# Hybrid decoder trunk on one core: new step offsets for the phases of sliding attention and retention

## The chip, the cores and the metric

The kernel runs on one core of a Trainium2 chip. The metric is the device time of one execution in microseconds (us). Before the change the median of three runs is 1740.38 us (1739.54 to 1740.76). One more execution was profiled.

## What is computed

Two decoder layers over 512 tokens of width 1024. Each layer is a SwiGLU block, a hybrid mixer and a second SwiGLU block, each followed by a residual sum and a layer norm. The change lies in the mixer, which projects its input once into seven parts and feeds two groups of heads:

```python
def hybrid_mixer(x, w_in, w_out, sinks, rope_cos, rope_sin, ret_cos, ret_sin):
    h = x @ w_in
    qa, ka, va, qr, kr, vr, gr = jnp.split(h, IN_SPLITS, axis=-1)
    ...
    y_attn = sliding_window_sink_attention(qa, ka, va, sinks)   # 8 query heads, 2 key heads of 64
    ...
    y_ret = multiscale_retention(qr, kr, vr, gr)                # 8 heads of 64
    return jnp.concatenate([y_attn, y_ret], axis=-1) @ w_out
```

Sliding attention works on blocks of 128 tokens: a token group of 128 queries sees its own block and the one before it, masked to a window of 128 keys. Its softmax has a learned sink per head:

```python
m = jnp.maximum(jnp.max(s, axis=-1, keepdims=True), sink)
p = jnp.exp(s - m)
denom = jnp.sum(p, axis=-1, keepdims=True) + jnp.exp(sink - m)
o = jnp.einsum('bnhgqk,bnkhd->bnqhgd', (p / denom).astype(v.dtype), vv)
```

Retention is chunked by 128 tokens: decayed scores within a chunk, a state carried from chunk to chunk, a norm per head, and a gate.

## The kernel before

**Matmuls.** Every large matmul is done in three: each fp32 operand is split into a high and a low part (`split`, ScalarE writes the high part at line 175, VectorE the low part at line 176), and `mm3` (lines 190 to 192) adds high by high, high by low and low by high in one PSUM bank. These three lines are nearly all of TensorE's work. In the mixer they are the projections: `proj` gives a transposed projection of 512 tokens in 24 matmuls, `proj_tok` a projection of 128 tokens with 512 columns, also in 24.

**Steps.** The mixer's program is traced in one order by Python, and two kinds of work are woven together by a counter. `projs` and `proj_tok` call `self.step()` after each 12 matmuls, in the middle and at the end of a projection. `step` adds one to `now` and runs each waiting task whose time has come. A task is a generator; `yield w` sets its next time to `now + w`. `spawn(gen, delay)` sets its first. Within one step the tasks run in the order in which they were spawned. `finish` runs tasks to their end at once.

**Attention tasks.** After the first value projection of retention (line 947) four tasks are spawned, one for each token group n. A task has these phases:

- scores (line 1043): 24 matmuls with 64 rows of the array each, in four PSUM banks; then copies and masks into the tile `s` (lines 1046, 1048) and the softmax of the first key head (lines 1053 to 1066), all traced in the same step
- the softmax of the second key head, after the `yield` of line 1067 (3 steps)
- transposes (line 1073), after the same `yield`'s second turn (4 steps): 8 of 128 by 128 in two PSUM banks, with masks at line 1076
- values (line 1087), after the `yield` of line 1081 (2 steps): 8 matmuls with 64 columns of weights (4 for group 0) in one PSUM bank, then a split into `yah`, `yal`

**Retention tasks.** Four tasks for pairs of heads. Task p is spawned when its rotated queries and keys have been traced (line 962), with the delay `STEPS[p][0]`. Its phases on TensorE are the scores (line 1101, 16 matmuls with 64 rows) with key transposes (line 1112), then after `STEPS[p][1]` steps the states (line 1122, 6 matmuls, which read the decayed keys that VectorE wrote at line 1115), then after `STEPS[p][2]` steps the outputs (lines 1139 and 1135). The last phase, two steps later, works on VectorE and GpSimd alone and writes `O` (line 1159).

**What the end of the mixer waits for.** After the gate projections the output projection begins with the attention half of token groups 0 and 1 (`half(0, 0)`, `half(1, 0)`). The retention half of group 0 needs `O` times the gates (line 977), its transposes (line 490) and their split.

**What sets the order.** A scheduler lays out each engine's instructions by tracing order and readiness at build time. The splits and the `mm3` matmuls are kept behind the instruction that was traced before them on their engine; the matmuls of the tasks aren't. So the first projection matmul behind a step stands behind the last TensorE instruction that the step traced. Everything waits by semaphores. There are eight PSUM banks of one kind (`ps`), given out to projections and tasks alike. The tiles `s`, the transposed weights and the queries share a pool of eight (`t4k`), retention's tiles a pool of ten (`rr`).

Of the kernel before, what the change touches and what calls it, by code (L numbers as in the profile page):

```python
# [22 lines left out]
NT = SEQ // P  # L23
# [12 lines left out]
AHEAD = 8  # L36
LOOK = 6
DELAY = (5, 5, 9, 9)
STEPS = ((4, 2, 2), (3, 2, 3), (3, 3, 2), (3, 2, 2))

QA, KA, VA, QR, KR, VR, GR = 0, 512, 640, 768, 1280, 1792, 2304

# [57 lines left out]
class Trunk:  # L100
# [772 lines left out]
    def mixer(self, sinks, cst, g, b):  # L873
        nc, tc, W = self.nc, self.tc, self.W
        with ExitStack() as ctx:
# [64 lines left out]
            att, ret = [], []  # L940
            us = [W.get() for _ in range(4)]
            for t in range(NT):
                acc = self.ps()
                self.proj_tok(acc, us, t)
                if t == 0:
                    for n in range(NT):
                        att.append(self.spawn(self.attention(n), 5 * n))
                nc.scalar.copy(vr[:, t, :], acc)
            W.done(4)
            for pp in range(2):  # L950
                kq = [[None, None], [None, None]]
                for i in range(2):
                    for cc in range(2):
# [6 lines left out]
                        if i:  # L960
                            p = pp * 2 + cc
                            ret.append(self.spawn(self.retention(p, kq[cc][1], kq[cc][0]), STEPS[p][0]))

# [60 lines left out]
    def attention(self, n):  # L1024


        nc = self.nc
        c = self.c
        k0 = max(n - 1, 0) * P
        nk = (n + 1) * P - k0  # L1030
        nb = nk // P
        ns = slice(n * P, (n + 1) * P)
        mm = nc.tensor.matmul
        s = self.big([P, 8, P])
        over = c["over"].bitcast(mybir.dt.int32)[:, None, :].to_broadcast([P, 2, P])
        for c2 in range(2):
            sb = [self.ps().rearrange("p (c k) -> p c k", c=2) for _ in range(2)]
            q, k = self.qT[c2], self.kT
            for cc in range(2):
                for i, (qi, ki) in enumerate(((0, 0), (0, 1), (1, 0))):  # L1040
                    for kv in range(2):
                        pr = slice(kv * HD, (kv + 1) * HD)
                        mm(sb[kv][:, cc, :nk], q[qi][pr, cc, ns], k[ki][pr, k0 : k0 + nk], start=i == 0, stop=i == 2)  # L1043
            for kv in range(2):
                h0 = kv * 4 + c2 * 2
                nc.scalar.copy(s[:, h0 : h0 + 2, :], sb[kv][:, :, nk - P : nk])
                ahead = sb[kv][:, :, :P] if n else c["rsc"][:, 3:4, 4:5].to_broadcast([P, 2, P])
                nc.vector.copy_predicated(s[:, h0 : h0 + 2, :], over, ahead)
        for kv in range(2):
            hs = slice(kv * 4, kv * 4 + 4)  # L1050
            den = self.small.tile([P, 4], F32, tag="den", name=self.nm("den"))
            m = self.small.tile([P, 4], F32, tag="m", name=self.nm("m"))
            nc.vector.tensor_reduce(out=m, in_=s[:, hs, :], op=ALU.max, axis=AX.X)
            nc.vector.scalar_tensor_tensor(out=m, in0=m, scalar=-SCALE, in1=c["nsk"][:, hs], op0=ALU.mult, op1=ALU.min)
            es = self.small.tile([P, 4], F32, tag="es", name=self.nm("es"))
            nc.vector.tensor_add(es, m, c["sk"][:, hs])
            for cc in range(4):
                h = kv * 4 + cc
                nc.scalar.activation(s[:, h, :], s[:, h, :], AF.Exp, bias=m[:, cc : cc + 1], scale=SCALE,
                                     accum_out=den[:, cc : cc + 1])  # L1060
            nc.scalar.activation(es, es, AF.Exp)
            nc.vector.tensor_add(den, den, es)
            nc.vector.reciprocal(den, den)
            for cc in range(4):
                h = kv * 4 + cc
                nc.scalar.activation(s[:, h, :], s[:, h, :], AF.Copy, scale=den[:, cc : cc + 1])
            yield 3 + kv
        pT = []
        for kv in range(2):
            pT.append(self.big([P, 2, 512]))  # L1070
            tb = self.ps()
            for cc in range(4):
                nc.tensor.transpose(tb[:, cc * P : (cc + 1) * P], s[:, kv * 4 + cc, :], self.ident)  # L1073
            if n:
                for kb, mask in enumerate(("under", "causal")):
                    nc.vector.tensor_tensor(out=pT[kv][:, kb, :].rearrange("p (c q) -> p c q", c=4),
                                            in0=tb.rearrange("p (c q) -> p c q", c=4),
                                            in1=c[mask][:, None, :].to_broadcast([P, 4, P]), op=ALU.mult)
            else:
                nc.scalar.copy(pT[kv][:, 0, :], tb)  # L1080
        yield 2
        yb = self.ps()
        for kb in range(nb):
            blk = n - nb + 1 + kb
            for kv in range(2):
                cs = slice(kv * HD, (kv + 1) * HD)
                mm(yb[cs, :], self.va[:, blk, cs], pT[kv][:, kb, :], start=kb == 0, stop=kb == nb - 1)  # L1087
        self.split(self.ya[0][:, :, ns], self.ya[1][:, :, ns], yb.rearrange("p (c q) -> p c q", c=4))

    def retention(self, p, qT, kT):  # L1090
# [19 lines left out]
        for n in range(NT - 1):  # L1110
# [6 lines left out]
                                in1=wk[:, None, hp, None].to_broadcast([P, NT - 1, 2, HD]), op=ALU.mult)  # L1117
        yield STEPS[p][1]
        kvb = self.ps()
# [6 lines left out]
        for n in range(1, NT - 1):  # L1126
            nc.vector.scalar_tensor_tensor(out=st[:, n, :], in0=st[:, n - 1, :], scalar=g128[:, p : p + 1],
                                           in1=st[:, n, :], op0=ALU.mult, op1=ALU.add)
        yield STEPS[p][2]
        ob = self.ps()  # L1130
# [131 lines left out]
```

## Time and profile before

| | |
|---|---|
| median of three runs | 1740.38 us |
| profiled execution | 1738.96 us |
| its span, first to last instruction | 1737.2 us |
| mean granted TensorE clock | 0.999 |
| DMA, mean over the span | 126 GB/s |
| matmuls of lines 190 to 192 in the chain of work that ended last | 31% each |

Busy shares of the engines stand in the prediction. The chain of work that ended last is followed back from the last instruction: its pieces follow each other without a gap, so each piece's duration is what that piece costs the kernel, and groups of equal matmuls are given as one piece ("x8"). "PE ps L190" is a matmul of line 190 into a PSUM tile. A row of the timeline shows the start, the duration, the engine, the line, the operation and its tiles, and in brackets the idle time before it and what ended that. The list of waits shows who waited for whom: the sum in us, how often, the longest.

### The profile page before, as it was taken

Reading aid. Unit: us, or ns where it says so; the run is one execution under the profiler, and the core shown is the slowest. Engines: PE = TensorE matmul, PEld = TensorE weight load, DVE = VectorE, ACT = ScalarE, POOL = GpSimd, SP = SyncE. Lnnn points to the kernel's source line nnn. Section 1 sums busy time; section 2 is a strip of 40 time slices with the busy share of each in tenths; the row PEclk is TensorE's granted clock in tenths of the full one; section 3 lists DMA queues with packets and bytes.
Section 4 is the critical chain, followed back from the end, with each engine's and each line's share of the span. In section 5 each row is a group of like instructions: output and inputs, shape, how many; then the busy total and the mean of one; then the engine's idle time right before and its main releaser. Section 6 shows DMA issues by size and latency. Waiting matters only on the chain.

```text
span 1737.2 us, 29495 instructions
## 1 busy us (share of the span) xinstructions
PE 1726.2 (99%) x11998; PEld 1574.6 (91%) x11998; DVE 1432.8 (82%) x2041; ACT 965.4 (56%) x1587; POOL 189.7 (11%) x160
## 2 busy tenths in 40 slices
PE   9999999999999999999999999999999999999998
PEld 9999988897788999998899999889877899999886
DVE  7888888856867999878999988888568589888887
ACT  5465656378623655565555556554784246555651
POOL 0000022111211000014010000312011110000231
PEclk9999999999999999999999999999999999999999
DMA  6334389422223243279433324982323133334891
GB/s 194 98 98 138 130 205 203 132 86 80 67 97 74 98 143 101 98 216 214 139 74 130 114 98 158 214 198 92 106 77 98 49 94 126 98 109 137 212 211 49
DMA packets 167223, 219.52 MB, mean 126 GB/s; under 512 B 5296, under 2 KB 119984, under 8 KB 167088
## 3 DMA queue, kind: packets, MB, share of 16 engines
q1 hardware_dynamic: 142160, 172.55, 30.5%
q0 software_dynamic: 24928, 45.09, 14.5%
q8 instruction: 94, 1.54, 0.4%
q14 instruction: 41, 0.34, 0.1%
HBM read 212.38 MB, written 2.10 MB: 123 GB/s over the span
## 4 chain that ended last, share of the span: by engine, by line
PE 98%; DMA 1%; DVE 1%; ACT 0%; SPq 0%; POOLq 0%; issue 0%; DVEq 0%
PE ps L190 31%; PE ps L191 31%; PE ps L192 31%; PE ps L490 1%; DMA raw<-in_ffn_w_gu_dram 1%; PE ps L1087 1%; PE ps L1043 1%; PE ps L1139 1%; PE ps L1101 1%; PE ps L1073 0%; PE ps L1135 0%; PE ps L1122 0%; PE ps L462 0%; PE ps L1112 0%; DVE ul L176 0%; ACT uh L175 0%
## 5 line engine op out<-in xcount | busy, mean ns | idle before, releaser
L190 PE MATMUL ps<-xh,uh 128*128 128x256 f32 (+1 forms) x1544 | 449.6, 291 | 0.0
L192 PE MATMUL ps<-xh,ul 128*128 128x256 f32 (+1 forms) x1544 | 447.5, 290 | 0.4 <-DVE ul L176 0.4
L191 PE MATMUL ps<-xl,uh 128*128 128x256 f32 (+1 forms) x1544 | 447.3, 290 | 0.4 <-DVE xl L176 0.4
L175 ACT CAST uh<-raw 128x1024 fp32r<-128x1024 f32 (+1 forms) x274 | 234.2, 875 | 204.6 <-PE ps L191 102.5
L192 PE MATMUL ps<-Th,ul 128*128 128x256 f32 x1248 | 345.0, 276 | 0.0
L190 PE MATMUL ps<-Th,uh 128*128 128x256 f32 x1248 | 345.0, 276 | 0.0
L191 PE MATMUL ps<-Tl,uh 128*128 128x256 f32 x1248 | 345.0, 276 | 0.0
L176 DVE TENSOR_TENSOR ul<-raw,uh 128x1024 fp32r<-128x1024 f32 (+1 forms) x274 | 270.2, 1003 | 65.0 <-ACT uh L175 64.0
L190 PEld LDWEIGHTS ps<-xh,uh 128*128 128x128 f32 x1544 | 290.1, 188 | 8.6 <-issue 1.6
L192 PEld LDWEIGHTS ps<-xh,ul 128*128 128x128 f32 x1544 | 290.1, 188 | 8.2 <-DVE ul L176 0.9
L191 PEld LDWEIGHTS ps<-xl,uh 128*128 128x128 f32 x1544 | 291.0, 189 | 7.0 <-DVE xl L176 0.6
L190 PE MATMUL ps<-uh,xh 128*128 128x512 f32 x720 | 285.4, 396 | 0.5 <-ACT xh L175 0.5
L191 PE MATMUL ps<-ul,xh 128*128 128x512 f32 x720 | 282.9, 393 | 0.0
L192 PE MATMUL ps<-uh,xl 128*128 128x512 f32 x720 | 281.3, 391 | 0.0
L192 PEld LDWEIGHTS ps<-Th,ul 128*128 128x128 f32 x1248 | 234.4, 188 | 0.0
L191 PEld LDWEIGHTS ps<-Tl,uh 128*128 128x128 f32 x1248 | 234.4, 188 | 0.0
L190 PEld LDWEIGHTS ps<-Th,uh 128*128 128x128 f32 x1248 | 234.4, 188 | 0.0
L175 ACT CAST uh<-S 128x1024 fp32r<-128x1024 f32 x156 | 163.5, 1051 | 119.6 <-PE ps L191 110.0
L176 DVE TENSOR_TENSOR ul<-S,uh 128x1024 fp32r<-128x1024 f32 x156 | 190.5, 1223 | 35.1 <-ACT uh L175 34.8
L396 POOL DMA_DIRECT2D R<-in_ffn_w_down_dram x80 | 96.4, 1211 | 993.8 <-DVE ul L176 898.6
L176 DVE TENSOR_TENSOR ul<-R,uh 128x1024 fp32r<-128x1024 f32 x120 | 145.4, 1224 | 29.3 <-ACT uh L175 28.8
L175 ACT CAST uh<-R 128x1024 fp32r<-128x1024 f32 x120 | 124.8, 1047 | 71.6 <-DMA R<-in_ffn_w_down_dram 33.7
(160 smaller groups left out, 2430.7 us busy)
## 6 DMA issues: line engine op xcount, KB each, us to landing
raw<-in_ffn_w_gu_dram SPq DMA_DIRECT2D x86, 1024.0 KB, 5.8
R<-in_ffn_w_down_dram POOLq DMA_DIRECT2D x80, 512.0 KB, 7.5
raw<-in_w_in_dram SPq DMA_DIRECT2D x18, 1024.0 KB, 5.2
R<-in_ffn_w_down_dram SPq DMA_DIRECT2D x16, 1024.0 KB, 6.5
raw<-in_ffn_w_down_dram SPq DMA_DIRECT2D x12, 1024.0 KB, 7.7
R<-in_ffn_w_down_dram SPq DMA_DIRECT2D x8, 512.0 KB, 4.2
raw<-in_w_in_dram SPq DMA_DIRECT2D x8, 512.0 KB, 5.9
raw<-in_w_out_dram SPq DMA_DIRECT2D x8, 512.0 KB, 6.2
```

The source lines that it names most:

```text
L175: a = self.nc.scalar.copy(hi, src)
L176: b = self.low = self.nc.vector.tensor_sub(lo, src, hi.bitcast(F32))
L190: keep(mm(out, ah, bh, start=start, stop=False, **kw))
L191: keep(mm(out, ah, bl, start=False, stop=False, **kw))
L192: keep(mm(out, al, bh, start=False, stop=stop, **kw))
L396: self.nc.gpsimd.dma_start(src, rows(i, j, g * 2, 2), accum_op=ALU.add))
L490: nc.tensor.transpose(b[:, c * P : (c + 1) * P], src[:, c * P : (c + 1) * P], self.ident)
L1043: mm(sb[kv][:, cc, :nk], q[qi][pr, cc, ns], k[ki][pr, k0 : k0 + nk], start=i == 0, stop=i == 2)
L1087: mm(yb[cs, :], self.va[:, blk, cs], pT[kv][:, kb, :], start=kb == 0, stop=kb == nb - 1)
L1101: nc.tensor.matmul(sb[:, ns], kT[pr, ns], qT[pr, ns], start=True, stop=True)
L1139: ins = nc.tensor.matmul(ob[:, o0 : o0 + HD], ST[h][:, n, :], vr[:, n, p * P + h * HD : p * P + (h + 1) * HD], start=n == 0, stop=n == 0 o ...
```

## The change

The change edits four places, all of them numbers of steps:

```diff
-STEPS = ((4, 2, 2), (3, 2, 3), (3, 3, 2), (3, 2, 2))
+STEPS = ((5, 2, 2), (5, 2, 3), (4, 2, 2), (4, 2, 2))
...
                     for n in range(NT):
-                        att.append(self.spawn(self.attention(n), 5 * n))
+                        att.append(self.spawn(self.attention(n), 5 * n + 1))
...
-            yield 3 + kv
+            yield 2 + kv
         pT = []
...
-        yield 2
+        yield 5 if n < NT - 1 else 3
         yb = self.ps()
```

Attention's task n now starts at step 5n + 1 after the spawn, its second softmax follows two steps later, the transposes three after that, and the values five steps after the transposes, for the last group three. (Task 0 starts at step 1 either way, since a delay of 0 is seen by the next step only.) So from step 11 on the values of one group, the transposes of the next and the scores of the one after stand in one step. Retention's tasks 0, 2 and 3 start one step later, task 1 two; task 2 has two steps instead of three to its states. No instruction is added or removed.

## The prediction

> **What bounds the kernel now.** I read the page's busy shares first, then the chain of work that ended last, then the list of TensorE's waits, and last the chain inside the two mixer stages (372 to 530 us, and 1231 to 1390 us for layer 1), piece by piece.
>
> ```profile
> span 1737.2 us, 29495 instructions
> PE 1726.2 (99%) x11998; PEld 1574.6 (91%) x11998; DVE 1432.8 (82%) x2041; ACT 965.4 (56%) x1587; POOL 189.7 (11%) x160
> PE 98%; DMA 1%; DVE 1%; ACT 0%; SPq 0%; POOLq 0%; issue 0%; DVEq 0%
> PE ps L190 <- ACT xh L175: 0.5, 2, 0.2
> ```
>
> TensorE is busy 99% of the span and carries 98% of the chain. The only wait of TensorE that is charged to a mixer stage is the last row: 0.5 us, twice 0.2, at the first use of the gated retention output. So a mixer stage lasts as long as its matmuls take to stream, and the change, which removes no matmul, can act in two ways only: through what it costs TensorE to go from one kind of matmul to another, or through a wait that isn't there today.
>
> The profiled execution took 1738.96 us around its span of 1737.2 us; the median of the runs shown is 1740.38 us, 1.4 us more. I work out differences and add them to the median.
>
> **Where the groups stand.** One step is half a projection, 12 matmuls of lines 190 to 192. I counted steps from the spawn of the attention tasks (line 947), by hand, through `step`, and write S, T, V for the scores, transposes and values of a token group, A, B, C for retention's three TensorE phases (lines 1101 with 1112; 1122; 1135 with 1139).
>
> Before: S0 1, S1 5, T0 8, V0 S2 10, T1 12, V1 14, S3 15, A0 16, T2 A1 17, B0 18, V2 B1 19, C0 20, T3 C1 22, A2 23, V3 24, A3 25, B2 26, B3 27, C2 28, C3 29. That is 20 interruptions of the projections' stream a layer, and the chain below shows them in this order. After: S0 1, T0 S1 6, V0 T1 S2 11, V1 T2 S3 16, A0 17, B0 A1 19, V2 T3 C0 B1 21, V3 C1 A2 24, B2 A3 26, C2 B3 28, C3 30. That is 11. Inside a step the older task goes first, as V0 S2 and T2 A1 do now.
>
> **What an interruption costs.** Pieces of the chain (start, us on the chain, what), layer 0:
>
> ```profile
> 404.69 0.87 PE ps L1073 x8
> 405.57 0.24 PE ps L190
> 411.17 1.01 PE ps L1087 x4
> 412.18 1.63 PE ps L1043 x24
> 413.80 0.43 PE ps L190
> 426.08 1.87 PE ps L1087 x8
> 427.94 0.43 PE ps L190
> 430.94 1.63 PE ps L1043 x24
> 432.57 0.43 PE ps L190
> 435.57 1.09 PE ps L1101 x16
> 436.66 0.48 PE ps L1112 x3
> 437.14 0.24 PE ps L190
> 439.95 0.87 PE ps L1073 x8
> 440.82 1.09 PE ps L1101 x16
> 441.92 0.48 PE ps L1112 x3
> 442.39 0.23 PE ps L190
> 445.19 0.67 PE ps L1122 x6
> 445.86 0.23 PE ps L190
> 448.65 1.87 PE ps L1087 x8
> 450.52 0.86 PE ps L1122 x6
> 451.38 0.23 PE ps L190
> ```
>
> An undisturbed matmul of the stream takes 0.23. After T it takes 0.24, after A 0.24, after B 0.23: these groups leave nothing behind. After S and after V it takes 0.43, so each of these two costs 0.20 when the full array follows. Three shared steps exist already and show what sharing brings. T2 A1: 0.87, 1.09, 0.48, 0.23, each exactly what it is alone; sharing saved nothing. V2 B1: B takes 0.86 instead of 0.67, so V's 0.20 (here 0.19) moved from the stream's matmul to B; saved nothing. V0 S2: S takes its usual 1.63, and only one 0.43 follows; here 0.20 was saved, because V is followed directly by S, with no full-width matmul between.
>
> The Trainium skill, "TensorEngine Tiling (Array Packing)", section Key Properties, says that changing the tiling mode drains the TensorE. By that rule what counts is not interruptions but mode changes, and on my step lists these are 23 a layer before and 24 after, so the rule speaks against the change; the rows agree with it in kind (T and B, of full width, are free, V and S are not). Its sum would be that of the rows, one change more a layer.
>
> **The change part by part.** The four edits have one answer, since together they set the step list. *Attention (lines 947, 1067, 1081).* Exits from V or S to something else than S, at 0.20 each: before S0, S1, V0 S2 (one), V1, S3, V2, V3: seven. After: S0, S1, V0 to T1, S2, V1 to T2, S3, V2 to T3, V3 to C1: eight. The transposes stand between values and scores in the shared step, and take away the one direct neighbourship that there was: +0.20 a layer. V to T isn't in the trace; the nearest row is V to B, also full width, at 0.19, and the bounds are 0 and 0.20. I take 0.20. *Retention (line 39).* C leaves a small rest:
>
> ```profile
> 495.88 0.39 PE ps L1139 x4
> 496.27 0.29 PE ps L190
> ```
>
> 0.29 against 0.23 is 0.06 after C. Three of four C will be followed by B or A. Whether the 0.06 then disappears isn't shown; 0 to 0.18 a layer, and I take 0.05. Sum a layer +0.15, two layers +0.3; ends 0.0 and +0.4. No weight is taken or released at another step, so the loads of SP's queue and the splits of weights stay where they are; what moves besides matmuls is softmax, masks and retention's elementwise work on ACT and DVE, and one power of retention on POOL a task. That work is hidden behind the stream now, and stays so while the cover in each place below lasts.
>
> **Where a wait could come.** A matmul of the stream is pinned behind the last TensorE instruction that was traced, so a late group holds the stream.
>
> ```profile
> 428.06 1.28 ACT L1066 ACTIVATE b<-b,den 128x128 f32<-128x128 f32 x4 [1.27 <-DVE den L1063]
> 441.25 0.55 DVE L1115 TENSOR_TENSOR rr<-ps,rsc 128x384 f32<-128x384 f32 x1
> 505.75 2.50 DVE L977 TENSOR_TENSOR rr<-rr,O 128x512 f32<-128x512 f32 x4
> 509.99 0.45 PE ps L490 x4
> 414.37 0.69 DVE L176 TENSOR_TENSOR yal<-ps,yah 128x512 fp32r<-128x512 f32 x1
> 416.13 0.69 DVE L1020 TENSOR_TENSOR qk<-ps,retC 128x512 f32<-128x512 f32 x1 [0.39 <-ACT sw L1019]
> 444.28 0.69 DVE L1020 TENSOR_TENSOR qk<-ps,retC 128x512 f32<-128x512 f32 x1 [0.74 <-ACT sw L1019]
> ```
>
> (1) T2 waits for group 2's second softmax. It ended at 429.34, 15.5 us after S2's end (413.80). From S2 to T2 there are five steps now, not seven: 60 matmuls at 0.23 = 13.8, then V1 with its 0.20 (2.07) and half of T (0.44) = 16.3. Cover left 0.8 us, and the second softmax is issued one step earlier after its scores, which helps. (2) B0 waits for the decayed keys: ready at 441.80, 6.2 us after A0 began; B0 comes A0 (1.57) and two steps (5.5) = 7.1 after that start. Cover 0.9. (3) The transposes of the gated output wait for task 3: from C3's end (496.27) to the first product (505.75 + 0.69 = 506.44) are 10.2 us; today five steps (13.7) lie between, then four (11.0). Cover 0.8. (4) PSUM has eight banks, each group takes its own: V one, T two, S four, and the open projection one. V T S at step 11 needs all eight, with the previous projection's bank still read by its rotation. The eighth is due 2.75 (one step) + 1.01 + 0.20 + 0.87 + 0.8 (half of S) = 5.6 us after that projection's end. The rotation's last read of it ended 5.65 us after the end in the one row (416.82 against 411.17), and 9.4 us after it in the other (444.97 against 435.57). V0's bank comes free sooner, if it is the one given: 415.06 against V0's end at 412.18 is 2.9 us, and it is wanted 1.9 after. So a bank costs from nothing to 9.4 - 5.6 = 3.8 us a layer; I take nothing, as the row nearest to this place (5.65) is within 0.1 of the due time.
>
> These covers are thin, four of them, none negative. Forecast: 1740.38 + 0.3 = **1740.7 us**, no change; its own range is 1739.6 to 1742.0.
>
> **The rivals.** *Every interruption costs.* If each return to the stream is worth the 0.20 that S and V show, nine fewer in two layers save 3.6 us: 1736.8, faster by 0.21%. For it stands that all returns after S and V pay; against it that T, A and B return at 0.23 to 0.24 and that T2 A1 and V2 B1 saved nothing. Chance 0.06. The skill's "TensorE: Matmul & The Clock Gate", Part 3, lets a weight load overlap matmuls only when the row group differs, by which every group's first load, T's too, would stand open; the 0.87 of T with or without a neighbour disagrees.
>
> *A bank is late (slower).* The shared step of V, T and S takes all eight banks, and the last pair of scores, or the first projection matmul behind it, gets the bank whose rotation is read late. It decides from a lag over 5.6 us; at the longest lag seen it costs 3.8 a layer, 7.6 in all: 1748.3; to be slower by over 0.2% it takes 1.6 a layer. For it stands the row at 444.28, against it the row at 416.13, and that a freed bank of V or T can serve instead. Chance 0.12.
>
> *A thin cover breaks.* One of places 1 to 3 is 1 us late in each layer: +2.0 us, 1742.7, still within 0.2%. Chance 0.12, of which 0.02 is long enough to be slower.
>
> *The groups don't meet.* The order on TensorE is not pinned inside a step, so T may be laid behind S when its softmax is late. Then V meets S in steps 11 and 16, exits become six instead of seven, -0.2 a layer: 1740.0. Chance 0.08.
>
> **How the numbers follow.** Forecast 0.62, groups that don't meet 0.08, thin cover 0.12, late bank 0.12, every interruption 0.06. What a measurement of this kernel can tell from no change is about 0.2%, 3.5 us, so under 1736.9 is faster and over 1743.9 slower: faster 0.06, slower 0.12 + 0.02 = 0.14, the rest 0.80. The range is 1737.6 to 1744.2: it takes in the forecast, both small cases and the beginning of the late bank, and leaves out the first rival and most of the second, under 0.2.
>
> **What would show it.** In the changed profile's chain: 11 interruptions a layer; T at 0.87 between V and S with V's 0.20 on its first pieces; S at 1.63 behind T, then 0.43; B and A unchanged behind C; TensorE's busy time and instruction count the same. Wrong would be: a TensorE wait named for DVE or ACT at lines 1043, 1073, 1122 or 490 in the mixer that isn't the 0.2 of today; a stream matmul that waits for a rotation (lines 1019, 1020) or for `yal`; or groups that get shorter by 0.20 each when they share a step.

## The result and the profile after

| | before | after |
|---|---|---|
| median (6 runs each, side by side) | 1739.49 us | 1749.82 us |
| lowest to highest | 1738.54 to 1740.76 | 1748.43 to 1750.5 |
| profiled execution, its span | 1738.96, 1737.2 | 1748.43, 1746.7 |
| mean granted TensorE clock | 0.999 | 0.997 |
| S0's first matmul to the first of the gated output's transposes, layer 0 | 128.08 | 132.74 |
| the same, layer 1 | 128.08 | 132.76 |

The ratio is 1.0058 with an interval of 1.0047 to 1.0068: the change makes the kernel 0.58% slower. The prediction said no change. The last two rows are read from the starts in TensorE's timelines (layer 0: 381.75 to 509.83 before, 380.92 to 513.66 after). One execution of a kernel further below took 2903.84 us at a mean clock of 0.555 and is left out there.

First the page of the changed kernel: span, busy shares and the shares of the chain that ended last.

```profile
span 1746.7 us, 29519 instructions
PE 1730.2 (99%) x11998; PEld 1577.5 (90%) x11998; DVE 1433.7 (82%) x2041; ACT 966.5 (55%) x1587; POOL 190.7 (11%) x160
PE 90%; issue 6%; DVE 2%; DMA 1%; POOL 1%; ACT 0%; SPq 0%; POOLq 0%; DVEq 0%
```

The 11998 matmuls are the same, but TensorE is busy 4.0 us longer, and the span is 9.5 longer. TensorE carried 98% of the chain and carries 90% now. The rest is "issue", VectorE and GpSimd: the chain leaves TensorE somewhere. The list of TensorE's waits says where (who waited for whom: us in total, times, longest).

```profile
PE ps L190 <- DVE yal L176: 4.3, 2, 2.1
...
PE ps L1043 <- DVE qk L1020: 0.4, 2, 0.2
```

Neither row was there before. The first, twice 2.1 us, is one wait in each layer, of a projection matmul for `yal`, the low part of a token group's attention values. A stream matmul that waits for `yal` is one of the signs of being wrong that the prediction had named. The timeline of TensorE in layer 0 shows the place (start, duration, what, and in brackets the idle time before).

```profile
431.28 1.94 PE L1087 MATMUL ps<-b,va 128*64 128x512 f32 x8
433.15 1.09 PE L1073 MATMUL ps<-ident,b 128*128 128x128 f32 x8
434.17 1.10 PE L1043 MATMUL ps<-qk,b 64*128 64x256 f32 x13
435.45 0.97 PE L1043 MATMUL ps<-qk,b 64*128 64x256 f32 x11 [0.18 <-DVE qk L1020]
438.55 0.64 PE L190 MATMUL ps<-xh,uh 128*128 128x512 f32 x1 [2.13 <-DVE yal L176]
```

This is step 16, and it falls at the end of a projection: V1, T2, S3, and then the first matmul of the next projection. V takes one bank, T two, S four. The projection that has just ended holds one, and the one before it, which ended two steps earlier, holds one as well, since the copies for its rotation run only from 432.33 on (below). That makes nine where there are eight: S3's last bank is the rotated one, which is the small wait of 0.18 for line 1020. The next projection, at 438.55, wants a tenth. Its matmul reads the input and a weight (`xh,uh`), not `yal`; what can tie it to `yal` is the bank that `yal` is computed from, V1's. The profile names no banks, so this is inferred here; the experiments test it. V1 ended at 433.22 (431.28 + 1.94), and its bank was read for the last time at 438.50, 5.28 us later.

Why it was read so late stands in the timelines of the two engines that read it. ScalarE:

```profile
432.33 2.35 ACT L1019 COPY sw<-ps 32x512 f32<-32x512 f32 x4
434.70 1.05 ACT L175 CAST uh<-raw 128x1024 fp32r<-128x1024 f32 x1
435.77 1.17 ACT L1019 COPY sw<-ps 32x512 f32<-32x512 f32 x2
436.96 0.59 ACT L175 CAST yah<-ps 128x512 fp32r<-128x512 f32 x1
```

VectorE:

```profile
434.70 0.69 DVE L1020 TENSOR_TENSOR qk<-ps,retC 128x512 f32<-128x512 f32 x1 [2.32 <-ACT sw L1019]
436.07 0.69 DVE L1022 TENSOR_TENSOR qk<-qk,sw 128x512 f32<-128x512 f32 x1 [0.68 <-POOL sw L1021]
436.68 1.22 DVE L176 TENSOR_TENSOR ul<-raw,uh 128x1024 fp32r<-128x1024 f32 x1
437.81 0.68 DVE L176 TENSOR_TENSOR yal<-ps,yah 128x512 fp32r<-128x512 f32 x1
```

The first half of the split, `yah`, stands on ScalarE behind six copies for rotations and a weight's cast; the second, `yal`, on VectorE behind a rotation's sum and the same weight's low part. The matmul starts as `yal` ends.

The wait isn't all. The view of busy times by stretches, around the wait and after it (columns: stretch and its length; busy time and number of instructions of PE, PEld, DVE, ACT, POOL; then the granted clock, DMA share, GB/s):

```profile
436.40:438.55 2.15, 0.02 (x1) 0.00 (x0) 2.15 (x4) 2.09 (x4) 0.00 (x0) 1.00 1.03 215
438.75:442.17 3.42, 3.42 (x9) 2.67 (x9) 3.42 (x9) 2.24 (x5) 1.29 (x1) 0.50 0.04 7
442.17:446.00 3.83, 3.83 (x31) 2.98 (x30) 3.83 (x10) 1.75 (x9) 0.00 (x0) 1.00 0.00 0
```

For 3.4 us after the wait the clock is 0.50, and the stream's matmuls take 0.43 us instead of 0.23. Eight of them cost 8 x 0.20 = 1.6. Layer 1 shows the same from 1302.33 on. So far the reading: about 2.1 of waiting and 1.6 of half clock, of the 132.74 - 128.08 = 4.66 us that a layer's stretch became longer. Both layers make 9.3 of the 9.5 us by which the span grew.

### The profile page after: what moved, and what is told of

Same layout as the page of the kernel before. It is cut to its first block, busy times and chain, and to the rows that moved or that the text cites. A ratio compares the mean times of both kernels' runs of the same rounds, so it can differ in the third digit from the quotient of the medians.

```text
span 1746.7 us, 29519 instructions
## 1 busy us (share of the span) xinstructions
PE 1730.2 (99%) x11998; PEld 1577.5 (90%) x11998; DVE 1433.7 (82%) x2041; ACT 966.5 (55%) x1587; POOL 190.7 (11%) x160
## 4 chain that ended last, share of the span: by engine, by line
PE 90%; issue 6%; DVE 2%; DMA 1%; POOL 1%; ACT 0%; SPq 0%; POOLq 0%; DVEq 0%
PE ps L191 28%; PE ps L190 28%; PE ps L192 28%; PE ps L490 1%; DMA raw<-in_ffn_w_gu_dram 1%; POOL sw L1021 1%; PE ps L1139 1%; DVE ul L176 1%; PE ps L1101 1%; PE ps L1087 0%; PE ps L1135 0%; PE ps L1122 0%; DMA retS<-c_retS_dram 0%; PE ps L462 0%; ACT sw L1019 0%
```

## The experiments

The theory: V1's bank is wanted while its readers are queued behind other work, and the half clock follows from the wait. The rivals: retention's new steps; the values, late because of the softmax; a cost of several groups in one step as such. The kernel before was timed beside every run; ratios are against it, with their 95% interval.

**Each half of the change alone.** In the changed kernel, retention's steps as before:

```diff
-STEPS = ((5, 2, 2), (5, 2, 3), (4, 2, 2), (4, 2, 2))
+STEPS = ((4, 2, 2), (3, 2, 3), (3, 3, 2), (3, 2, 2))
```

> The change's three attention edits alone; retention's STEPS as before the change. Bank theory (V1, T2 and S3 in one step take all eight PSUM banks with the open projection's, the next projection waits about 2.1 us for the bank that V1 filled, and the clock that is halved afterwards costs another 1.6 us, in each layer): the wait is still there, and longer, since A0 falls into step 16 too and wants three banks more: 1747 to 1756 us, a TensorE wait of 2 us or more a layer at line 190 or 1101. Retention theory (the tasks moved later crowd VectorE and ScalarE): 1739 to 1741 us, no such wait. Late-softmax theory (T2, five steps behind S2 instead of seven, holds the stream): 1747 to 1750.

Measured: 1752.04 us, ratio 1.0070 (1.0053 to 1.0087). TensorE's waits in this kernel:

```profile
PE ps L1101 <- DVE yal L176: 4.3, 2, 2.1
...
PE ps L1101 <- DVE b L1076: 1.3, 2, 0.8
```

Attention's steps alone bring the whole loss. The wait for `yal` is as long as in the changed kernel, but another instruction has it: A0, retention's first scores, which fall in step 16 here and come before the projection. Retention's scores don't read `yal` either; whoever wants the next bank waits.

The other half: the kernel before, with retention's new steps only.

```diff
-STEPS = ((4, 2, 2), (3, 2, 3), (3, 3, 2), (3, 2, 2))
+STEPS = ((5, 2, 2), (5, 2, 3), (4, 2, 2), (4, 2, 2))
```

> Retention's STEPS of the change alone; attention as before the change. Bank theory: V, T and S never meet, no wait of over 0.5 us, clock full: 1739 to 1741 us. Retention theory: most of the loss is here, 1746 to 1750. Late-softmax theory: 1739 to 1741.

Measured: 1739.63 us, ratio 0.9999 (0.9989 to 1.0008), no new wait. Retention is out of it.

**All values one step earlier.** In the changed kernel:

```diff
-        yield 5 if n < NT - 1 else 3
+        yield 4 if n < NT - 1 else 3
```

> The changed kernel with the values of groups 0 to 2 four steps behind their transposes instead of five, so at steps 10, 15 and 20, one step ahead of the shared one. T and S still share theirs, at the same distances from the scores. Bank theory: one bank less is wanted in steps 11 and 16 and V1's is read by then; no wait of over 0.5 us, clock full: 1740 to 1742 us. Late-softmax theory: T2 is where it was, so 1748 to 1751. Retention theory: 1748 to 1751.

Measured: 1741.18 us, ratio 1.0007 (0.9997 to 1.0016). No wait for `yal`, no half clock. The values read the softmax's result and its transposes; they come earlier and wait for nothing, and T2, at the step it has in the changed kernel, doesn't wait either, so a late softmax isn't the cause. This kernel parts V from T and S in every step, however, so it doesn't tell the bank from the company.

**One group's values one step earlier.** Only V1 is moved; V0 T1 S2 and V2 T3 C0 B1 still share their steps.

```diff
-        yield 5 if n < NT - 1 else 3
+        yield (5, 4, 5, 3)[n]
```

> The changed kernel with the values of group 1 alone one step earlier, at step 15; V0 T1 S2 and V2 T3 still share their steps. Bank theory: the 2.1 us wait at step 16 and the half clock behind it go, in both layers, and nothing else does: 1749.8 - 2 x (2.1 + 1.7) = 1742.2 us. Rival, that the shared steps cost by themselves: a third to a half of the loss stays, 1744 to 1747.

Measured: 1742.59 us, ratio 1.0015 (1.0006 to 1.0024). The chain of waits in this kernel at step 16 (start, us on the chain, what):

```profile
435.09 0.12 PE ps L1073
435.21 0.56 ACT sw L1019
...
435.79 0.58 ACT sw L1019
...
436.39 0.70 DVE qk L1020
...
437.14 0.97 PE ps L1043 x10
438.12 0.43 PE ps L190
438.55 0.23 PE ps L191
```

The first projection matmul follows the scores at once, and the clock is full: 0.43 is what S leaves behind, 0.23 the undisturbed matmul. V1's bank is free by now, and one move of 12 matmuls of the stream took 7.2 us off the time (1749.82 to 1742.59). In the trace the layer's stretch is 129.00 long, 3.74 less than in the changed kernel: the wait of 2.13 and the half clock's 1.6. The move also parts V1 from T2 and S3; but V0, T1 and S2 still share step 11 here, and the rest worked out below is far too small for company as such to be the cause. What is left of the shortage is in this chain too: S3's last bank is the one that the rotation (lines 1019, 1020) reads.

The rest of the loss can be read from the same stretch in three kernels: 129.00 here, 128.50 in the kernel with all values a step earlier, 128.08 before. About one half of the 0.5 between the first two is at this step: T2 and S3 take 3.03 here (435.09 to 438.12) and 0.87 + 1.91 = 2.78 in the chain of the other. The other half is at step 11, which V0 T1 S2 share here as in the changed kernel. TensorE's timeline of the changed kernel:

```profile
413.04 1.08 PE L1087 MATMUL ps<-b,va 128*64 128x512 f32 x4
414.05 1.09 PE L1073 MATMUL ps<-ident,b 128*128 128x128 f32 x8
415.08 2.08 PE L1043 MATMUL ps<-qk,b 64*128 64x256 f32 x24
```

TensorE's weight loads for these scores in the changed kernel, second part:

```profile
416.18 0.77 PEld L1043 LDWEIGHTS ps<-qk,b 64*128 64x128 f32 x11 [0.21 <-DVE qk L1020]
```

and the scores' matmuls in the kernel with all values a step earlier:

```profile
416.86 1.69 PE L1043 MATMUL ps<-qk,b 64*128 64x256 f32 x24
```

S2 takes 2.08 behind V0 and T1, and 1.69 where V0 came a step earlier: 0.39 more, with a wait for the rotation's read (line 1020) inside the group, which the other kernel doesn't have. Against it stands the 0.20 that V0 costs by itself there. The last 0.42 against before are mainly the 0.20 for V0, which no longer stands directly before S2, and S3, 1.91 instead of 1.63 in the chain.

**The bank read sooner, at the same step: two tries.** In the changed kernel, first the split on VectorE alone, no longer kept behind the instruction traced before it:

```diff
-        self.split(self.ya[0][:, :, ns], self.ya[1][:, :, ns], yb.rearrange("p (c q) -> p c q", c=4))
+        hi, lo = (v[:, :, ns] for v in self.ya)
+        yv = yb.rearrange("p (c q) -> p c q", c=4)
+        nc.vector.tensor_copy(hi, yv)
+        nc.vector.tensor_sub(lo, yv, hi.bitcast(F32))
```

> The changed kernel, but the high part of the attention output's split is written by VectorE instead of ScalarE, where it waited behind the rotation's copies for 3.8 us after V1's end. Every group stays at its step. Bank theory: V1's bank is read within 2 us of V1's end, the wait of 2.1 us at the projection behind S3 goes, and with it the half clock: 1740.5 to 1742.5 us. Late-softmax and retention theories: nothing changes, 1748 to 1751.

Measured: 1746.14 us, ratio 1.0038 (1.0023 to 1.0053): about 4 us less than the change, not the 8 or so expected. VectorE's timeline in this kernel:

```profile
436.38 0.68 DVE L1090 CAST yah<-ps 128x512 fp32r<-128x512 f32 x1
436.99 0.68 DVE L1076 TENSOR_TENSOR b<-ps,under 128x512 f32<-128x512 f32 x1
437.58 0.68 DVE L1091 TENSOR_TENSOR yal<-ps,yah 128x512 fp32r<-128x512 f32 x1
```

The edit swapped one queue for another: `yah` now stood behind the rotation's sum on VectorE, and a mask of the transposes came between the two halves. The wait went from 2.1 to 1.8 us. The clock accounts for the rest: the four executions took 1744.08, 1745.69, 1746.59 and 1748.76 us, at mean clocks of 0.999, 0.998, 0.998 and 0.996. The first of them is the traced one, and after both waits of 1.8 us its clock stays full. That the half clock came in others is inferred from their times and mean clocks; they weren't traced.

Second, the same split on both engines, with high priority in the scheduler:

```diff
+        with self.tc.high_priority():
+            nc.scalar.copy(hi, yv)
+            nc.vector.tensor_sub(lo, yv, hi.bitcast(F32))
```

> The changed kernel, every group at its step, but the split that reads the values' bank is put ahead of what was traced before it on ScalarE and VectorE. Bank theory: the bank of V1 is read within 2 us of V1's end; wait and half clock gone: 1741 to 1743 us. Rival (shared steps cost by themselves): 1748 to 1750.

Measured: 1750.08 us, ratio 1.0057 (1.0038 to 1.0075), the wait for `yal` again twice 2.1. ScalarE's timeline shows that the order stayed as it was:

```profile
435.55 1.05 ACT L175 CAST uh<-raw 128x1024 fp32r<-128x1024 f32 x1
436.62 1.17 ACT L1019 COPY sw<-ps 32x512 f32<-32x512 f32 x2
437.81 0.59 ACT L1091 CAST yah<-ps 128x512 fp32r<-128x512 f32 x1
```

So this run says nothing about an earlier read, and whether step 16 could be kept with one stays open.

**What a pause of TensorE costs.** In the kernel before, the first matmul of the third token group's first projection (line 943's loop) is held until GpSimd has done a few small instructions on a tile; nothing of the computation changes. The lines in `mm3` that hold the matmul, and the table `PAUSE` with the numbers of instructions, aren't shown here.

```diff
+                if t == 2:
+                    w, h = self.small.tile([P, 8], F32, tag="pause", ...), self.mhalf
+                    for i in range(PAUSE[self.mixers]):
+                        self.hold = nc.gpsimd.tensor_mul(w, w if i else h, w if i else h)
...
+                        self.hold = nc.gpsimd.tensor_tensor(out=w, in0=w, in1=h, op=ALU.pow)
```

> The kernel before, in which one projection matmul of the first stretch (the third token group's, where no group stands between) waits for a GpSimd chain that starts behind the matmul before it: one multiply and one power of 128x8 in layer 0 (about 1.9 us), two of each in layer 1 (about 3.8 us). No bank is short here. Idle theory (TensorE's own idle time lowers the granted clock to half for 3.4 us): layer 1 shows half clock, 1.7 us more than its pause; layer 0 may or may not, since 1.8 us did not lower it in one profile and 2.1 us did in another. Rival (the groups of small matmuls ahead of the wait count as idle, the wait alone does nothing): full clock in both layers. Time by the idle theory 1740 + 1.9 + 3.8 + 1.7 = 1747, with a second drop 1749; by the rival 1746.

Measured: 1774.61 us in a single execution, far over what the pauses cost. Two things lie in it. The wanted one, stretches before and after the pause, layer 0 and then layer 1:

```profile
392.70:395.10 2.40, 0.35 (x2) 0.00 (x0) 0.52 (x4) 2.36 (x11) 1.85 (x2) 1.00 0.02 7
396.10:399.40 3.30, 3.30 (x9) 2.52 (x9) 0.34 (x2) 1.65 (x10) 0.00 (x0) 0.50 0.02 5
1268.00:1272.20 4.20, 0.17 (x1) 0.00 (x0) 0.34 (x2) 4.17 (x20) 3.69 (x4) 1.00 0.00 0
1273.30:1276.70 3.40, 3.40 (x10) 2.64 (x9) 0.00 (x0) 0.00 (x0) 0.00 (x0) 0.50 0.02 5
```

An idle time of 2.07 us in the one layer and of 4.06 in the other are each followed by a half clock that lasts 3.413 us in both: here twice the idle time doesn't make it longer. The unwanted part is told in the last section. A second form without a tile of its own, with one shorter pause:

```diff
-                    w, h = self.small.tile([P, 8], F32, tag="pause", ...), self.mhalf
+                    w, h = self.small.tile([P, 8], F32, tag="gmu", ...), self.mhalf
```

> As the pause run, in the same place, but without a tile of its own (the pause tile takes a place of an existing kind, so that no address moves), with four GpSimd multiplies in layer 0 (about 1.2 us of idle TensorE) and one multiply and one power in layer 1 (about 2.2 us). Idle theory with its point between 1.8 and 2.1 us: full clock in layer 0, half clock for 3.4 us in layer 1. If idle of any length lowers the clock: half clock in both. Time 1739.8 + 1.2 + 2.2 + 1.7 = 1745; if it is 1770 or more, the pause run's extra 25 us were not due to its tile.

Measured: 1746.18 us in a single execution, beside 1739.85. The waits in this kernel, and the stretches behind them:

```profile
PE ps L193 <- POOL gmu L957: 2.1, 1, 2.1
...
PE ps L193 <- POOL gmu L953: 1.2, 1, 1.2
```

```profile
387.80:392.00 4.20, 4.18 (x18) 3.48 (x19) 0.68 (x4) 3.51 (x16) 0.00 (x0) 1.00 0.02 4
...
1251.10:1254.40 3.30, 3.30 (x10) 2.52 (x9) 0.34 (x2) 1.93 (x11) 0.00 (x0) 0.50 0.02 5
```

After 1.2 us the clock stays full, after 2.1 us it is halved, without any change of the attention's steps and with no group of small matmuls in the 2.9 us ahead of the wait. An idle time of 2.1 us is enough for the half clock.

**What the change could have won.** V directly before S saves the 0.20 between them. In the kernel before, the values are moved next to other groups without the transposes between:

```diff
-        yield 2
+        yield (2, 3, 6, 3)[n]
```

> The kernel before, with the values moved to directly ahead of another group of reduced width, and no transposes between: V1 to step 15 ahead of S3, V2 to step 23 ahead of A2, V3 to step 25 ahead of A3 (V0 stands ahead of S2 already). At most five banks in a shared step. Neighbour theory (V and S cost 0.20 us each when the full array follows, and nothing when S or A does): three exits fewer a layer, 0.6 us, 1.2 in all: ratio 0.9993, 1738.8 us where before is 1740.0. Rival, that sharing a step with S or A costs by itself: 1 to 4 us slower.

Measured: 1741.04 us, ratio 1.0005 (0.9996 to 1.0013). Each of the three new neighbourships saves 0.2, by the starts in TensorE's timelines: V1 and S3 with the return to the stream take 3.69 instead of 2.07 + 1.83 = 3.90, V2 A2 and V3 A3 3.43 each instead of 2.06 + 1.56 = 3.62. But V2 had stood before B1 and covered the decayed keys. TensorE's waits in this kernel:

```profile
PE ps L1122 <- DVE rr L1115: 1.6, 2, 0.8
```

0.8 us a layer of waiting at B1 takes the 0.6 back and more: the layer's stretch is 128.63 instead of 128.08. With B1 a step later as well:

```diff
-STEPS = ((4, 2, 2), (3, 2, 3), (3, 3, 2), (3, 2, 2))
+STEPS = ((4, 2, 2), (3, 3, 2), (3, 3, 2), (3, 2, 2))
...
-        yield 2
+        yield (2, 3, 6, 3)[n]
```

> The kernel before with V1, V2, V3 moved ahead of S3, A2, A3 as in the run with the values before the scores, and retention's task 1 given three steps instead of two to its states, since B1 lost the cover of V2 there and waited 1.0 us a layer for its decayed keys. Neighbour theory: no new wait of over 0.3 us, three exits of 0.20 us fewer a layer, 1.2 us less in all than before: 1738.6 where before is 1739.8, ratio 0.9993. Rival (a shared step costs by itself, or the next thin cover breaks): at or over before's time.

Measured: 1739.6 us, ratio 0.9995 (0.9986 to 1.0004). The layer's stretch is 127.77 instead of 128.08, so 0.31 of the 0.6 remain, 0.6 us in all: right in sign in the trace, and too little to be told from no change by the times.

## Why the prediction was wrong

**The steps and what the groups cost: right.** The chain of the changed kernel shows the 11 interruptions in the listed order. Two of them, steps 21 and 24:

```profile
458.18 1.87 PE ps L1087 x8
460.04 1.02 PE ps L1073 x8
461.07 0.39 PE ps L1139 x4
...
463.47 0.72 PE ps L1122 x6
...
472.50 1.87 PE ps L1087 x8
474.37 0.59 PE ps L1139 x4
...
476.97 1.09 PE ps L1101 x16
```

T behind V takes 1.02 instead of 0.87, and C behind V 0.59 instead of 0.39: V's cost moves to the next group of full width. It is 0.15 to 0.20 there, within the bounds of 0 and 0.20. A layer pays V0's exit anew, and 0.04 to 0.05 less for each of V1 and V2. B behind C takes 0.72 instead of 0.67, so there C's rest moves; A behind C takes its usual 1.09, so there it disappears. The 0.05 taken for that was about right, and too small to matter. "Every interruption costs" is refuted by these rows: what a group left to the stream moves to the next group, and nine interruptions fewer saved nothing.

**The thin covers 1 to 3: held.** No wait for a softmax, for the decayed keys or for the gated output was added. The cover that was called 0.8 to 0.9 was enough in all three.

**The bank (cover 4): the step that failed.** The prediction priced step 11, and put a bank at nothing since the one lag of 5.65 us was within 0.1 of the due time there, and since V0's bank, read 2.9 us after its end, could serve instead (though by the prediction's own figures it was wanted after 1.9). Both were taken over to step 16 without a look at what the readers do there. V1's bank was read 5.28 us after its end, 2.4 later than V0's in the kernel before. It was named as a rival, with the right victim ("the first projection matmul behind it") and the wrong bank: the rotation's was foreseen as the late one, and a freed bank of V as the way out. At step 16 that way out was the late one. The place was priced wrong besides: step 11 lies in the middle of a projection, step 16 at the end of one, where the next projection wants a tenth bank, and this has no term in the sum. What the runs showed in place of the nothing: 2.13 us of waiting a layer for that tenth bank, and 0.39 and some 0.5 inside S2 and S3 for the rotation's.

**The clock: not in the sum at all.** The rival's 3.8 us a layer were meant as pure waiting. At the next projection the loss was 2.1 of waiting, and 1.6 that follow from it. That the rival's 1748.3 lies near the measured 1749.82 is partly chance: its wait was too long, and the half clock was missing.

**Chances and range.** The row quoted for the rival, a lag of 9.4 us at 444.28, was as good a sample as the one against it, two rows in all, for an event in either of two steps of both layers. Such a pair can't carry 0.12 against 0.62. The range left out most of that rival.

| per layer | predicted | measured |
|---|---|---|
| exits and C's rest | +0.15 | 0 to +0.1 |
| bank at step 11, inside S2 | 0 | +0.4 |
| bank at step 16, inside S3 | 0 | +0.5 (434.17 to 436.42 is 2.25, against 1.70 before) |
| bank at step 16, next projection | 0 | +2.13 |
| half clock behind it | not in the sum | +1.6 |
| sum of the rows | +0.15 | +4.6 to +4.7, where the stretch shows +4.66 |

## What to carry to other kernels

When groups are gathered into one step, count the PSUM banks of all of them and of the stream's next tile, and look up for each bank that is to be given on when its last reader runs, on that engine and at that step: the reader's place in its queue decides, not the length of the read. A gathering saved here only where two groups of reduced shape (V and S, V and A) became direct neighbours (0.2 us), and a group that is moved away may have been the cover of the one behind it. And price a wait of TensorE of about 2 us here as nearly twice its length, because of the clock.

## What the runs showed of the hardware

**The clock falls after a short idle time.** In these traces 1.2 us of idle left the clock full, and so did two waits of 1.8 us. All nine of 2.06 us or more (the longest 4.06) were followed by half clock: seven times for 3.413 us, 1.6 us of time, and twice for 6.827 us. Both of these were in layer 0 behind a wait of 2.1 us, with attention's steps alone and with the split at high priority; the row of the latter:

```profile
438.63:445.46 6.83, 6.06 (x18) 4.48 (x20) 6.83 (x16) 4.29 (x13) 1.29 (x1) 0.50 0.13 26
```

In every trace the times between two changes of the clock are whole multiples of 3.413 us (in the changed kernel 127, 1, 252, 1 and 128 of them). So the clock changes at fixed marks, and where an idle time falls between the marks may count beside its length; by what rule stays open. The Trainium skill, "TensorE: Matmul & The Clock Gate", Part 1, lists the half clock as the state after at least one idle window of about 3.4 us. By that a wait of 2.1 us would leave the clock alone; the traces here disagree, and only the 3.413 us is the page's.

**A kernel with one small tile more had slower matmuls.** The first pause kernel, in its single execution, has 25 us beyond its pauses (1774.61 - 1739.76 = 34.9, less 6.1 of waiting and 2 x 1.6 of half clock). The list of groups in that kernel (columns: busy us, mean ns):

```profile
L193 PE MATMUL ps<-Th,uh 128*128 128x256 f32 x1248 | 351.1, 281 | 0.0
```

and in the kernel before:

```profile
L190 PE MATMUL ps<-Th,uh 128*128 128x256 f32 x1248 | 345.0, 276 | 0.0
```

These matmuls stand in the SwiGLU blocks, far from the pause, and are 5 ns longer each; from start to start it is 118.4 against 113.4 ns in the mean, some 18 us over the 3744 of the three lines. The first pause kernel has a tile of 32 bytes a partition that the second hasn't, and in the second, with other lengths of its pauses but without the tile, the time is gone (276 ns again). That the addresses behind the tile moved, and that this is the cause, is inferred, not shown.
